# Request, selection and accumulator stores moved in the seam before the first expert of a hybrid encoder layer

## The chip, the cores and the metric

The kernel runs on one core of a Trainium2 chip. Its engines work side by side, each through its own list of instructions, and wait for one another through semaphores: PE (TensorE, the matrix multiplications), DVE (VectorE) and ACT (ScalarE, both elementwise), POOL (GpSimd, used here for small work and for transfers whose rows are chosen by an index), and SP (SyncE, which does nothing here but issue transfers). The profile lists PE's weight loads apart as PEld. The metric is the device time of one execution in microseconds (us), lower is better; where several runs are given, their median counts.

## The reference

One layer of an encoder on 1024 tokens of width 1024, in float32. A mixer (a retention, a state-space and a windowed attention head group) is followed by a layer norm, a layer of 16 experts that choose their tokens, and a second layer norm:

```python
mix = concat(retention, s5, attention) @ w_out
h = layer_norm(ALPHA * h + mix, ln1_g, ln1_b)         # "H1" below
ffn = expert_choice_ffn(h, router_w, w_gate, w_up, w_down)
h = layer_norm(ALPHA * h + ffn, ln2_g, ln2_b)

def expert_choice_ffn(x, router_w, w_gate, w_up, w_down):
    cap = EC_FACTOR * seq // N_EXPERTS                 # 128 tokens for each expert
    aff = softmax(x @ router_w)                        # tokens x 16 experts
    gates, idx = lax.top_k(aff transposed, cap)        # each expert takes its best 128
    xs = x[idx]
    hdn = silu(xs @ w_gate) * (xs @ w_up)              # 128 x 2048
    out = (hdn @ w_down) * gates
    return zeros.at[idx].add(out)                      # summed by token
```

## The kernel before

The tokens are eight tiles of 128 rows (0 to 7; the code calls 7 `LT`, the last tile). A front of some 448 us computes the mixer and the first norm tile by tile; the experts follow, one after another, each in four quarters of its 2048 hidden columns.

**What sets the order.** The whole kernel is scheduled by hand. A table, `ENDS` (for the last tiles; `PLACES` for the others), gives each step a due time, and `F.at(zero + place, step)` sorts the steps by it. Each engine then takes its instructions in that order. The numbers are due times of the plan, not times of the trace: they set an order and nothing else. Transfers that SP issues keep this order too.

**The norm's end of each tile.** For tile `t` the normed rows `z` are written to DRAM twice: as they are, by `out_proj_store` (`H1`, L1727: `h_d<-z`), from where the experts fetch their tokens; and times ALPHA, by `out_proj_scale` on ACT (`AH`, L1734: `ah<-z`) and `out_proj_scaled` (`AD`, L1738: `acc_d<-ah`), as the start of the accumulator to which the experts add. The buffers come from pools. Tag `z` of pool `op` has three places. In this stretch they hold in turn rows of the last tiles, the `ah` of tiles 6 and 7 and the candidates' rows `xc`. Tile 7's mean and gain are computed in halves (`GH`, `SJ`), and its power (`PW`, L1601 on POOL) gives the reciprocal deviation from which both its rows and its softmax follow.

**The first expert's tokens without a search.** Experts 1 to 15 get their tokens by a search (`top_k`, with L2212 among its lines), which takes long and runs on DVE between the other work of the first expert. Expert 0 gets its own by counting. Of tiles 0 to 6 the best 128 tokens are found ahead of tile 7 ("candidates"): their numbers give an index (`CI`, `candidates_index`, L2106), and POOL fetches their rows by it (`XC`, `candidates_rows`, L2111: `z<-h_d,cindex`, into `xc`). When tile 7's affinities are there, each candidate counts how many of tile 7's tokens go ahead of it (`RD7`, L2046 on DVE; `PC`, `first_counts`, L2153 on PE; `LP` and `U1`, L2169 and L2173 on DVE), and each token of tile 7 gets its rank (`RR`, `LR`, `U0`: L2046, L2049, L2161, L2165 on DVE). `U1` and `U0` leave in `rows` two 128x128 matrices of zeros and ones, `K.hits[1]` for the candidates and `K.hits[0]` for tile 7. `first_turned` (`FZ` with tile 7's rows `z`, `FX` with `xc`) multiplies rows and hits on PE into two halves of PSUM, and so both selects and transposes the expert's tokens: `tp<-rows,z`, two halves of four blocks by two sources, 16 multiplications in all (the trace has two records for each). ACT copies the halves to `xF` (`X0`, `first_tokens`, L2445), which PE multiplies with the first gate weights; `xT`, split in two parts, follows. Between the steps on which PE waits, `idle` puts multiplications whose result nobody reads (`FILL` says behind which step and how many).

**The experts' weights** come in pieces of 1 MB (128x2048). For each quarter SP loads two pieces of the gate, two of the up, and two of the down matrix of the quarter before. Most pieces go to `wraw` (`X.load`, L2379) and are split into a high part by ACT (L2417) and the rest by DVE (L2426), from which PE makes three multiplications in place of one; pieces 0, 1, 4, 5, 10 and 11 go whole to `whole` (`X.load_whole`, L2404) and are multiplied unsplit. `RL` are the loads of pieces 2 and 3, `up` of the first quarter, in the order's words two `wraw<-in_exp_w_up`; `W4` those of 4 and 5.

**Memory taken over.** When the front is done its pools are closed, among them `op` (with tag `z`) and `tk`; in the same memory `ex`, `raw2` and `sel` are opened. `raw2` takes the weight loads from piece 8 on in part, `sel` holds the search's buffers `w`, which two COPY of DVE fill (L2212: `w<-tp`). Whoever writes first into such a buffer waits until the front's instructions, transfers included, that read or wrote that memory are done.

Of the kernel before, what the change touches and what calls it, by code (L numbers as in the profile page):

```python
# [9 lines left out]
F32 = mybir.dt.float32  # L10
# [10 lines left out]
P = 128  # L21
L = 1024
D = 1024
NT = L // P
# [1358 lines left out]
def last_steps(K, last, spaces):  # L1383

    X = K.X
    last("XH", 0, fn=spaces[0], by=-0.0005)
    for i in range(2):
        last("XH", i, fn=lambda i=i: X.high(2 + i))
        last("XL", i, fn=lambda i=i: X.low(2 + i))
    for i in range(2):  # L1390
        last("RL", i, fn=lambda i=i: X.load(2 + i))
    for kind, k in (("W0", 0), ("W4", 4)):
        last(kind, fn=lambda k=k: X.load_whole(k))
    for kind, fn in (("CP", candidates_counts), ("CQ", candidates_sums), ("CR", candidates_ranks), ("CH", candidates_hot),
                     ("CF", candidates_numbers), ("CC", candidates_keep), ("CI", candidates_index),
                     ("XC", candidates_rows), ("CA", candidates_half), ("CB", candidates_share), ("CT", candidates_parts),
                     ("CK", candidates_turn), ("CW", candidates_row), ("TS", silu_table), ("R7", first_row),
                     ("RD7", first_before), ("PC", first_counts), ("RR", first_own), ("LR", first_sum), ("U0", first_hits),
                     ("LP", first_place), ("U1", first_hits_row), ("HB", first_parts)):
        last(kind, fn=lambda fn=fn: fn(K))  # L1400
    last("R7", fn=spaces[1], by=-0.0005)
    K.halves = {}
    for half in range(2):
        last("FZ", half, fn=lambda half=half: first_turned(K, half, 0))
        last("FX", half, fn=lambda half=half: first_turned(K, half, 1))
        last("X0", half, fn=lambda half=half: X.first_tokens(half, K.halves[half]))
    last("FX", 1, fn=lambda: setattr(K, "numbers", first_numbers(K)), by=0.0005)
    for half in range(2):
        last("GH", half, fn=lambda half=half: out_proj_gain(K, LT, half))
        last("SJ", half, fn=lambda half=half: out_proj_shift(K, LT, half))  # L1410
    for kind, n in FILL:
        last(*kind, fn=lambda n=n: idle(K, n), by=0.0004)
# [303 lines left out]
def out_proj_gain(K, t, half=None):  # L1716
    z, cs = out_proj_columns(K, t, half)
    K.nc.vector.scalar_tensor_tensor(z, z, K.mr[t][0], K.g1[:, cs], op0=OP.subtract, op1=OP.mult)


def out_proj_shift(K, t, half=None):
    z, cs = out_proj_columns(K, t, half)
    K.nc.vector.scalar_tensor_tensor(z, z, K.mr[t][1], K.b1[:, cs], op0=OP.mult, op1=OP.add)
# [5 lines left out]

def out_proj_scale(K, t):  # L1730

    late = t >= NT - 2
    K.ah[t] = K.op.tile([P, D], F32, name="ah", tag="z" if late else "rt", bufs=3 if late else 1)
    K.nc.scalar.activation(K.ah[t], K.Y[t][2], AF.Copy, scale=ALPHA)  # L1734


def out_proj_scaled(K, t):
# [59 lines left out]
}  # L1797


FILL = ((("RP", 7, 1), 5), (("PC",), 3))  # L1800
ENDS = {
# [76 lines left out]
}  # L1878
# [2 lines left out]
def attention_steps(K, F, zero, out, qs, mat, spaces):  # L1881
# [26 lines left out]
    for c in range(NT):  # L1908
# [38 lines left out]
        for kind, fn in (("AF", router_logits), ("AE", router_exp), ("AG", router_shares), ("GN", out_proj_gain),  # L1947
                         ("SH", out_proj_shift), ("H1", out_proj_store), ("AH", out_proj_scale), ("AD", out_proj_scaled),
                         ("TK", token_parts), ("RK", rank_turn), ("RW", rank_keep), ("RB", rank_count)):
            if c < LT or kind in ("AF", "AE", "AG", "H1", "AH", "AD", "TK"):  # L1950
                at(c, kind, fn=lambda c=c, fn=fn: fn(K, c))
        if 0 < c < LT - 1:
            at(c, "CN", fn=lambda c=c: rank_sums(K, c))
            at(c, "CE", fn=lambda c=c: rank_sums_keep(K, c))
    last_steps(K, last, spaces)
    for k in range(2):
        F.at(zero + PERIOD * 4 + PLACES["LD"] + 0.01, lambda k=k: X.load(k))
# [50 lines left out]
LT = NT - 1  # L2008
# [166 lines left out]

def first_turned(K, half, i):

    if i == 0:
        K.halves[half] = K.ptp.tile([P, 4, P], F32, name="tp")
    src = (K.Y[LT][2], K.xc)[i]  # L2180
    for c in range(4):
        cs = slice((half * 4 + c) * P, (half * 4 + c + 1) * P)
        K.nc.tensor.matmul(K.halves[half][:, c, :], src[:, cs], K.hits[i], start=(i == c == 0), stop=(i == 1 and c == 3))


def first_parts(K):
# [5 lines left out]
def first_numbers(K):  # L2192

    nc, h = K.nc, K.hitb
    pt = K.ptp.tile([P, 4, P], F32, name="tp")
    nc.tensor.matmul(pt[:, 0, 0:5], h[0], K.tok[:, LT, 0, :], start=True, stop=False)
    nc.tensor.matmul(pt[:, 0, 0:5], h[1], K.cparts, start=False, stop=True)
    return pt
# [345 lines left out]
def idle(K, n):  # L2544

    ps = K.pmm.tile([P, 512], F32, name="gu" if K.pmm is K.__dict__.get("pg") else "mm")
    for i in range(n):
        K.nc.tensor.matmul(ps, K.X.whl[2][:, 0, 0:P], K.X.whl[2][:, 0, 0:512], start=True, stop=True)
# [300 lines left out]
```

## Time and profile before

| | |
|---|---|
| runs of the kernel, median of 3 | 1564.23 us (1562.92 to 1564.55) |
| profiled execution | 1562.62 us |
| its span in the trace | 1560.9 us |
| instructions | 21150 |
| read from memory, written | 461.75 MB, 42.99 MB |
| mean rate over the span | 323 GB/s |
| largest group, PE L2334 `gu<-whl,xT` | 3000 multiplications, 712.5 us busy |
| split of the weights, DVE L2426 | 378, 860.5 us busy, 2288 ns each |
| split of the weights, ACT L2417 | 378, 725.3 us busy, 1919 ns each |

Busy time is the time in which an engine worked, a weight load of PE beside its multiplications apart. A busy share alone says little where the stages have different limits; the chain of waits, followed back from the last instruction, says which engine's work could not have been later. A row of the timeline has the start in us, the busy time, the engine, the line, the operation with output and inputs, and, in brackets, the idle time ahead of it and who ended it. SPq and POOLq are the two queues' issues of transfers, and behind an issue stands the median time to its landing.

### The profile page before, as it was taken

What the parts mean: (1) busy time and instruction counts of PE and PEld (TensorE: products, weight loads), DVE (VectorE), ACT (ScalarE), POOL (GpSimd) and SP (SyncE); (2) the same over time, 40 slices, a digit from 0 to 9 for tenths busy, and PEclk for the clock granted to TensorE, in tenths of its full rate; (3) what the DMA queues carried; (4) which work ended last, traced back from release to release, by engine and by line L of the source; (5) the groups of instructions that cost most, each with busy time, mean ns of one, the idle gap of its engine ahead of it and who ended that gap; (6) DMA issues with size and microseconds to landing.
All of it is one profiled execution on the core that took longest, in us unless ns stands there. A gap on an engine that the chain in (4) does not pass through costs nothing.

```text
span 1560.9 us, 21150 instructions
## 1 busy us (share of the span) xinstructions
PE 1543.1 (99%) x7710; PEld 1262.5 (81%) x7710; DVE 1401.8 (90%) x1720; ACT 1130.7 (72%) x1329; POOL 191.5 (12%) x248
## 2 busy tenths in 40 slices
PE   9999999999999999999999999999999999999997
PEld 7887887888767888888888888888888888888886
DVE  7987965889989999999999999989999999999996
ACT  7746556887736777777777777787877878787773
POOL 4002111111010001010010101000211201021121
PEclk9999999999999999999999999999999999999999
DMA  6556478353179999999999999999999999999992
GB/s 242 185 167 155 119 232 234 102 166 109 72 311 371 373 390 411 427 387 367 392 371 387 371 401 370 403 411 409 421 412 409 415 425 413 417 414 413 402 415 108
DMA packets 105177, 507.20 MB, mean 325 GB/s; under 512 B 16752, under 2 KB 29808, under 8 KB 54640
## 3 DMA queue, kind: packets, MB, share of 16 engines
q1 hardware_dynamic: 88624, 474.81, 77.6%
q0 software_dynamic: 16304, 30.94, 7.2%
q8 instruction: 61, 1.00, 0.2%
q14 instruction: 44, 0.36, 0.1%
q10 hardware_dynamic: 144, 0.09, 0.0%
HBM read 461.75 MB, written 42.99 MB: 323 GB/s over the span
## 4 chain that ended last, share of the span: by engine, by line
PE 90%; ACT 3%; DMA 3%; DVE 2%; issue 1%; POOL 1%; SPq 1%; POOLq 0%; ACTq 0%; DVEq 0%
PE gu L2334 44%; PE y L2334 22%; PE mm L64 4%; PE mm L66 4%; PE mm L65 4%; PE tp L2317 3%; PE gu L2342 1%; PE po L1525 1%; PE tp L1505 1%; DMA wraw<-in_w_out 1%; PE at L1454 1%; PE sm L265 0%; DMA uT<-in_x 0%; ACT S L1497 0%; PE at L699 0%
## 5 line engine op out<-in xcount | busy, mean ns | idle before, releaser
L2426 DVE TENSOR_TENSOR whl<-wraw,whl 128x2048 fp32r<-128x2048 f32 x378 | 860.5, 2288 | 61.1 <-ACT whl L2417 57.1
L2417 ACT ACTIVATE whl<-wraw 128x2048 fp32r<-128x2048 f32 x378 | 725.3, 1919 | 246.3 <-PE gu L2334 132.5
L2334 PE MATMUL gu<-whl,xT 128*128 128x512 f32 x3000 | 712.5, 394 | 0.0
L2334 PEld LDWEIGHTS gu<-whl,xT 128*128 128x128 f32 x3000 | 555.4, 188 | 114.8 <-issue 1.0
L2334 PE MATMUL y<-whl,hT 128*128 128x512 f32 x1536 | 359.4, 389 | 0.0
L2334 PEld LDWEIGHTS y<-whl,hT 128*128 128x128 f32 x1536 | 288.0, 188 | 59.7
L2295 POOL DMA_INDIRECT xs<-h_d,index x15 | 26.7, 1777 | 451.3 <-PE y L2334 304.1
L64 PE MATMUL mm<-hT,whl 128*128 128x512 f32 x160 | 65.3, 408 | 0.0
L66 PE MATMUL mm<-hT,whl 128*128 128x512 f32 x160 | 62.6, 391 | 0.0
L65 PE MATMUL mm<-hT,whl 128*128 128x512 f32 x160 | 62.5, 391 | 0.0
L64 PE MATMUL mm<-WO,yh 128*128 128x512 f32 x128 | 53.4, 418 | 0.0
L56 DVE TENSOR_TENSOR hT<-tp,hT 128x512 fp32r<-128x512 f32 x76 | 51.5, 683 | 1.9 <-ACT hT L55 1.7
L55 ACT ACTIVATE hT<-tp 128x512 fp32r<-128x512 f32 x76 | 43.7, 581 | 12.8 <-PE tp L206 6.7
L66 PE MATMUL mm<-WO,yl 128*128 128x512 f32 x128 | 50.6, 396 | 0.0
L65 PE MATMUL mm<-WO,yh 128*128 128x512 f32 x128 | 50.6, 395 | 0.0
L2468 DVE TENSOR_TENSOR hid<-hid,gu 128x512 f32<-128x512 f32 x64 | 43.5, 680 | 2.0 <-PE gu L2334 2.0
L64 PE MATMUL mm<-whl,hT 128*128 128x256 f32 (+1 forms) x120 | 42.4, 353 | 1.5 <-ACT gate L403 1.5
L2462 ACT ACTIVATE hid<-gu 128x512 f32<-128x512 f32 x64 | 37.1, 580 | 5.7 <-PE gu L2342 5.5
L66 PE MATMUL mm<-whl,hT 128*128 128x256 f32 (+1 forms) x120 | 40.2, 335 | 0.0
L65 PE MATMUL mm<-whl,hT 128*128 128x256 f32 (+1 forms) x120 | 40.0, 333 | 0.0
L1465 DVE CUSTOM_DVE_ANT_0 S<-at,R,sink 128x384 f32<-128x384 f32 (+1 forms) x64 | 36.8, 577 | 2.3 <-PE at L1454 1.7
L2317 PEld LDWEIGHTS tp<-ident,hid 128*128 128x128 f32 x256 | 31.8, 140 | 8.5 <-issue 0.5
(450 smaller groups left out, 1779.4 us busy)
## 6 DMA issues: line engine op xcount, KB each, us to landing
wraw<-in_exp_w_up SPq DMA_DIRECT2D x128, 1024.0 KB, 9.5
wraw<-in_exp_w_down SPq DMA_DIRECT2D x128, 1024.0 KB, 10.2
wraw<-in_exp_w_gate SPq DMA_DIRECT2D x122, 1024.0 KB, 9.2
wraw<-in_w_in SPq DMA_DIRECT2D x6, 1024.0 KB, 5.3
whole<-in_exp_w_gate SPq DMA_DIRECT2D x6, 1024.0 KB, 8.5
q_d<-kst SPq DMA_DIRECT2D x32, 128.0 KB, 2.6
wraw<-in_w_out SPq DMA_DIRECT2D x4, 1024.0 KB, 7.6
qs<-q_d POOLq DMA_DIRECT2D x16, 256.0 KB, 3.4
```

The costliest lines, as they stand in the source:

```text
L55: nc.scalar.activation(hi, src, AF.Copy)
L56: eng.tensor_tensor(lo, src, hi.bitcast(F32), OP.subtract)
L64: nc.tensor.matmul(ps, a[0], b[0], start=start, stop=False)
L65: nc.tensor.matmul(ps, a[0], b[1], start=False, stop=False)
L66: nc.tensor.matmul(ps, a[1], b[0], start=False, stop=stop)
L1465: K.nc.vector.tensor_tensor_reduce(S[g][:, :W], K.at.pop((i, g))[:, :W], K.R[:, ro:ro + W], 2.0 ** -(h + 1), K.sink[:, h:h + 1], OP.add, O ...
L2317: K.nc.tensor.transpose(pt[:, c, :], src[:, (c0 + c) * P:(c0 + c + 1) * P], K.ident)
L2334: nc.tensor.matmul(ps, a[s][c], u[:, t, i * w:(i + 1) * w], start=first and id(ps) not in began, stop=last and left[id(ps)] == 0)
L2417: self.K.nc.scalar.activation(u[:, 0, :], self.raw[k1].rearrange("p a b -> p (a b)"), AF.Copy)
L2426: self.K.nc.vector.tensor_tensor(u[:, 1, :], raw, u[:, 0, :].bitcast(F32), OP.subtract)
L2462: nc.scalar.activation(self.h[q], self.pg[q][0], AF.Silu)
L2468: at(self.after, q, 3, lambda: nc.vector.tensor_tensor(self.h[q], self.h[q], self.pg[q][1], OP.mult))
```

## The change

Four things move; no arithmetic is added or left out. (1) The request for the candidates' rows (`XC`) and its index (`CI`) go ahead of tile 7's power. (2) The candidates' count, place and hits go ahead of tile 7's rank on DVE, and PE multiplies the candidates first: `FX` opens each PSUM group and `FZ` closes it. One idle multiplication is left in place of three. (3) `AH` of tile 6 scales its rows in place instead of into a buffer of tag `z`, and its store goes behind tile 7's rows. (4) `AH` and `AD` of tile 7 go behind the loads `RL` and `W4`.

```diff
-    last("FX", 1, fn=lambda: setattr(K, "numbers", first_numbers(K)), by=0.0005)
+    last("FZ", 1, fn=lambda: setattr(K, "numbers", first_numbers(K)), by=0.0005)
...
 def out_proj_scale(K, t):
-    late = t >= NT - 2
-    K.ah[t] = K.op.tile([P, D], F32, name="ah", tag="z" if late else "rt", bufs=3 if late else 1)
+    if t == LT - 1:
+        K.ah[t] = K.Y[t][2]
+    else:
+        K.ah[t] = K.op.tile([P, D], F32, name="ah", tag="z" if t == LT else "rt", bufs=3 if t == LT else 1)
     K.nc.scalar.activation(K.ah[t], K.Y[t][2], AF.Copy, scale=ALPHA)
...
-FILL = ((("RP", 7, 1), 5), (("PC",), 3))
+FILL = ((("RP", 7, 1), 5), (("PC",), 1))
...
-    "AH": {6: 287.000, 7: 375.566},
-    "AD": {6: 315.900, 7: 378.895},
+    "AH": {6: 287.000, 7: 470.000},
+    "AD": {6: 336.001, 7: 470.100},
...
-    "XC": 335.142,
+    "XC": 279.500,
...
-    "FX": (378.883, 389.769),
+    "FX": (335.610, 335.620),
...
 def first_turned(K, half, i):
-    if i == 0:
+    if i == 1:
         K.halves[half] = K.ptp.tile([P, 4, P], F32, name="tp")
     src = (K.Y[LT][2], K.xc)[i]
     for c in range(4):
         cs = slice((half * 4 + c) * P, (half * 4 + c + 1) * P)
-        K.nc.tensor.matmul(K.halves[half][:, c, :], src[:, cs], K.hits[i], start=(i == c == 0), stop=(i == 1 and c == 3))
+        K.nc.tensor.matmul(K.halves[half][:, c, :], src[:, cs], K.hits[i], start=(i == 1 and c == 0), stop=(i == 0 and c == 3))
```

The other entries of `ENDS` that change (`CI`, `PC`, `LP`, `U1`) are seen in the order. The first place is DVE between tile 7's softmax (`aff<-aff,rsm`) and the first split of a weight piece; `G` and `cnt` are the comparisons and their counts, `last` the ranks, `rows` the hits. Before:

```order
L1708 TENSOR_SCALAR aff<-aff,rsm 128x16
L2046 TENSOR_SCALAR G,cnt<-rows,aff 128x128
L2046 TENSOR_SCALAR G,cnt<-tp,aff 128x128
L2049 SCALAR_TENSOR_TENSOR junk,cnt<-tp,aff,upto 128x128
L2161 TENSOR_REDUCE last<-cnt 128x1
L2165 TENSOR_SCALAR rows<-slots,last 128x128
L2169 SCALAR_TENSOR_TENSOR last<-tp,place 128x1
L2173 TENSOR_SCALAR rows<-slots,last 128x128
```

With the change, at the same place (the lines after it are two higher):

```order
L1708 TENSOR_SCALAR aff<-aff,rsm 128x16
L2048 TENSOR_SCALAR G,cnt<-rows,aff 128x128
L2171 SCALAR_TENSOR_TENSOR last<-tp,place 128x1
L2175 TENSOR_SCALAR rows<-slots,last 128x128
L2048 TENSOR_SCALAR G,cnt<-tp,aff 128x128
L2051 SCALAR_TENSOR_TENSOR junk,cnt<-tp,aff,upto 128x128
L2163 TENSOR_REDUCE last<-cnt 128x1
L2167 TENSOR_SCALAR rows<-slots,last 128x128
```

The candidates' place and hits moved ahead of tile 7's own four instructions. On POOL the request `z<-h_d,cindex` changed places with the power `l1rs<-l1rs,mhalf` and now stands ahead of it.

The second place is SP's list of transfers at the end of the front; the first row is tile 6's row store. Before:

```order
L1727 DMA h_d<-z 128x1024
L2404 DMA whole<-in_exp_w_gate 128x2048 x2
L1738 DMA acc_d<-ah 128x1024
L1727 DMA h_d<-z 128x1024
L1738 DMA acc_d<-ah 128x1024
L2379 DMA wraw<-in_exp_w_up 128x2048
L2404 DMA whole<-in_exp_w_gate 128x2048 x2
L2379 DMA wraw<-in_exp_w_up 128x2048
L2379 DMA wraw<-in_exp_w_down 128x2048 x2
```

With the change (tile 6's store now reads `z`, which it was scaled into):

```order
L1727 DMA h_d<-z 128x1024
L2406 DMA whole<-in_exp_w_gate 128x2048 x2
L1727 DMA h_d<-z 128x1024
L1740 DMA acc_d<-z 128x1024
L2381 DMA wraw<-in_exp_w_up 128x2048
L2406 DMA whole<-in_exp_w_gate 128x2048 x2
L2381 DMA wraw<-in_exp_w_up 128x2048
L1740 DMA acc_d<-ah 128x1024
L2381 DMA wraw<-in_exp_w_down 128x2048 x2
```

Tile 6's store went behind tile 7's row store, and tile 7's went from ahead of the four pieces of 1 MB to behind them.

The third place is DVE at the first two COPY of the search, with what they wait for; `w` are the search's buffers, `slotc` and `gates` the first expert's numbers. Each transfer has a semaphore that stands for it: SP's are DMAHW0 to DMAHW7 in turn, POOL's DMASW0 to DMASW7. In the program of before, the COPY's DMAHW4 is tile 7's store of L1738, DMAHW2 tile 6's, and DMAHW3 tile 7's row store. Before:

```order
L2307 TENSOR_TENSOR slotc<-slotc 128x1
L2308 TENSOR_TENSOR gates<-slotc 128x1 [waits DVE_49]
L2212 COPY w_5382<-tp 128x64 [waits DMAHW4_49,DMAHW5_49,DMAHW3_49,DMAHW6_49,DMAHW2_49,DMAHW7_49,DMASW4_49,PE_49]
L2212 COPY w_5384<-tp 128x64
L2215 MAX half_5386<-w_5382 128x8 [waits DVE_49]
```

With the change, DMAHW0 is tile 7's store of L1740, DMAHW3 tile 6's and DMAHW2 tile 7's row store:

```order
L2309 TENSOR_TENSOR slotc<-slotc 128x1
L2310 TENSOR_TENSOR gates<-slotc 128x1 [waits DVE_49]
L2214 COPY w_5379<-tp 128x64 [waits DMAHW3_49,DMAHW5_49,DMAHW2_49,DMAHW6_49,DMAHW0_49,DMAHW7_49,DMASW4_49,PE_49]
L2214 COPY w_5381<-tp 128x64
L2217 MAX half_5383<-w_5379 128x8 [waits DVE_49]
```

The COPY waits for tile 7's store in both programs; what moved is where that store stands on SP. SP's first load behind the store, `wraw<-in_exp_w_down`, waits for the same store in both.

8 rows, old and new, of the table ENDS are left out of this document.

## The prediction

> **What bounds the kernel now.** I read the page's busy times and its chain of waits, then the busy times by stretch, then the timelines of the five engines and the DMA landings around 440 to 480 us, where the change sits.
>
> ```profile
> PE 1543.1 (99%) x7710; PEld 1262.5 (81%) x7710; DVE 1401.8 (90%) x1720; ACT 1130.7 (72%) x1329; POOL 191.5 (12%) x248
> PE 90%; ACT 3%; DMA 3%; DVE 2%; issue 1%; POOL 1%; SPq 1%; POOLq 0%; ACTq 0%; DVEq 0%
> 600.00:700.00 100.00, 100.00 (x480) 82.18 (x479) 92.72 (x66) 76.75 (x55) 9.90 (x4) 1.00 1.01 405
> ```
>
> TensorE bounds it. In the last row (a stretch of the experts; the columns are the stretch, its length, busy PE, PEld, DVE, ACT and POOL, clock, DMA share, GB/s) PE has no free microsecond. So whatever PE loses before or early in the experts stays lost to the end, and whatever it gains is kept only if DVE (93%) and DMA (1.01) follow.
>
> The seam before the first expert, on PE and DVE:
>
> ```profile
> 442.63 0.18 PE L2153 MATMUL tp<-order,G 128*128 128x1 bf16 x1
> 442.68 1.45 PE L2548 MATMUL gu<-whl 128*128 128x512 f32 x3
> 444.06 4.09 PE L2183 MATMUL tp<-rows,z 128*128 128x128 f32 x32
> 448.04 3.68 PE L2342 MATMUL gu<-whole,xF 128*128 128x512 f32 x8
> 438.01 0.16 DVE L2116 TENSOR_TENSOR cand<-cand 128x1 f32<-128x1 f32 x1
> 438.28 0.15 DVE L2106 TENSOR_TENSOR cindex<-cand 128x1 uint32<-128x1 f32 x1
> 442.22 0.35 DVE L2046 TENSOR_SCALAR_CACHE_REDUCE G<-rows,aff 128x128 bf16<-128x128 f32 x1
> 443.71 0.29 DVE L2165 TENSOR_SCALAR rows<-slots,last 128x128 f32<-128x128 f32 x1
> 444.10 0.29 DVE L2173 TENSOR_SCALAR rows<-slots,last 128x128 f32<-128x128 f32 x1
> 445.09 0.75 DVE L1723 SCALAR_TENSOR_TENSOR z<-z,l1rs,b 128x512 f32<-128x512 f32 x1
> ```
>
> PE counts (442.63), fills with three idle multiplications, and starts the 16 selecting ones at 444.06, when the last tile's selection (443.71 + 0.29) is there. They take 4.0 us; the first expert starts at 448.04.
>
> **The candidates' rows and the selection (the gain).**
>
> ```profile
> 439.55 0.98 POOL L1601 TENSOR_TENSOR l1rs<-l1rs,mhalf 128x1 f32<-128x1 f32 x1 [6.45 <-DVE l1rs L1595]
> 440.72 1.08 POOL L2111 DMA_INDIRECT z<-h_d,cindex  x1 [0.18 <-DMA whole<-in_exp_w_gate]
> z<-h_d,cindex POOLq DMA_INDIRECT x1, 4.4
> L2295 POOL DMA_INDIRECT xs<-h_d,index x15: 938/1036/3062, 496.3 to 1396.8; - x15
> ```
>
> The index takes the slot at 438.01 instead of 438.28, and the gather no longer queues behind the power (439.55 to 440.53). It starts near 438.3, 2.4 us sooner, and with its 4.4 us lands near 442.7 instead of 445.1. POOL is free again at 438.3 + 1.08 = 439.4, just before the power's operand arrives at 439.5; I cost that at nothing. With the longest such request (3.06 us, third figure of the last row) the power would be 1.8 us late, and the softmax, queued on DVE behind it, too.
>
> Selecting the candidates first: the count ends at 442.81, the place and its selection follow on DVE and end near 443.4, so PE starts 0.6 us sooner (443.45 for 444.06). The last tile's selection comes 0.7 us later than now, about 444.4, behind eight multiplications that last to 445.4; its second half of rows (445.09 + 0.75 = 445.84) is needed near 446.5. Both are covered. The two idle multiplications that go were waiting time. But the clock (columns after the busy time: clock, DMA share, GB/s) was at half there:
>
> ```profile
> 440.38:440.50 0.12, 0.12 (x1) 0.50 0.00 0
> 443.75:443.88 0.12, 0.12 (x2) 0.85 0.80 328
> 1550.67:1551.10 0.43, 0.03 (x1) 1.00 0.00 0
> 1553.24:1553.66 0.43, 0.00 (x0) 0.50 0.00 0
> ```
>
> It fell near 440.4 and was back near 443.8, 3.4 us later, although the fillers ran. The 0.35 us from 443.45 to 443.8 at half speed give back 0.2, so the first expert starts **0.4 us sooner**, near 447.6.
>
> **The accumulator stores (the loss).** Tile 6's scaling in place costs the same 1.05 us; tile 7's now stands on ACT between xF and xT, and xT, 0.5 us later, is still done four microseconds before its first use. What counts is where the stores stand on SP's queue.
>
> ```profile
> 440.22 0.33 SPq L1738 DMA_DIRECT2D acc_d<-ah  x1
> 445.87 0.33 SPq L1727 DMA_DIRECT2D h_d<-z  x1
> 447.00 0.96 SPq L1738 DMA_DIRECT2D acc_d<-ah  x1
> 448.01 0.43 SPq L2379 DMA_DIRECT2D wraw<-in_exp_w_up  x1
> 449.89 0.66 SPq L2379 DMA_DIRECT2D wraw<-in_exp_w_up  x1
> 451.30 1.08 SPq L2379 DMA_DIRECT2D wraw<-in_exp_w_down  x2
> acc_d<-ah SPq DMA_DIRECT2D x1, 512.0 KB, 4.2
> wraw<-in_exp_w_up SPq DMA_DIRECT2D x1, 1024.0 KB, 13.3
> out<-zz SPq DMA_DIRECT2D x8, 512.0 KB, 9.3
> 445.92 1.06 ACT L1734 ACTIVATE ah<-z 128x1024 f32<-128x1024 f32 x1 [1.19 <-DVE z L1723]
> 448.19 0.60 ACT L2445 ACTIVATE xF<-tp 128x512 f32<-128x512 f32 x1 [0.72 <-PE tp L2197]
> 463.20 1.91 ACT L2417 ACTIVATE whl<-wraw 128x2048 fp32r<-128x2048 f32 x1 [5.50 <-DMA wraw<-in_exp_w_up]
> 465.84 1.91 ACT L2417 ACTIVATE whl<-wraw 128x2048 fp32r<-128x2048 f32 x1 [0.73 <-DMA wraw<-in_exp_w_down]
> ```
>
> Tile 7's store was issued at 447.00, ahead of four 1 MB loads, and landed 4.2 us later, at 451.2. Two things wait for that landing, because their buffers lie where the front's pools were: SP's next load (451.30) and the first COPY of the top-k search on DVE (the order's third place: its store semaphore is now DMAHW0). Now the store is issued only after all four loads, near 449.5 (ACT: second xF until 448.4, then 1.06). When does it land? The load issued at 449.89 landed 13.3 us later, at 463.2; it had the same bytes ahead of it as now (tile 6's store takes tile 7's place). With 0.5 MB more at 2.64 us per MB (463.20 to 465.84) the store lands 1.3 us behind it; up to 0.7 goes back because tile 6's store follows the row store at once: 463.8 to 464.5. As the loads behind it are now held back and do not share the engines, I take **463.5**. Ends: 449.5 + 4.2 = 453.7 if it landed as now, 449.5 + 9.3 = 458.8 as the late output stores do with loads ahead of them, and 464.5. It is nearest to the 13.3 us row, which is the same queue at the same moment.
>
> What stands behind the COPY:
>
> ```profile
> 451.87 0.22 DVE L2212 COPY w<-tp 128x64 f32<-128x64 f32 x1 [0.71 <-PE tp L2208]
> 460.79 0.69 DVE L2468 TENSOR_TENSOR hid<-hid,gu 128x512 f32<-128x512 f32 x1
> 465.14 2.29 DVE L2426 TENSOR_TENSOR whl<-wraw,whl 128x2048 fp32r<-128x2048 f32 x1 [2.03 <-ACT whl L2417]
> 464.02 0.60 PE L2317 MATMUL tp<-ident,hid 128*128 128x128 f32 x4
> 478.90 0.24 PE L2238 MATMUL tp<-ident,b 32*128 32x32 f32 x1
> ```
>
> From the COPY to the end of `hid` DVE works 451.87 to 461.48, 9.6 us, without a wait. PE transposes `hid` at 464.02: 2.5 us of slack, and the COPY comes 11.7 us later. PE starts that transpose at 463.5 + 0.1 + 9.6 + 0.1 = 473.3, **9.3 us later** than now (458.8 would give 4.6; 464.5, 10.3; 453.7, nothing). The 0.4 us gained are swallowed by this wait. Behind it DVE loses its 2.03 us idle at 465.14, so it is 9.6 us late at 478.90, no more than PE. The loads that SP holds go out at 463.6; the piece at 451.30 took 14.5 us to 465.84, so even so it is split by 482.3, and PE wants the rest of it near 484.
>
> PE idles from 463.6 to 473.3. At the end of the kernel the clock fell 2.5 us after PE's last work, and at 440.4 it took 3.4 us of work to return. I add half of 3.4, **1.7 us** (0 if it stays up, 3.4 if it takes two such spans).
>
> Sum: 9.3 + 1.7 = 11.0. The profiled execution took 1562.6 (span 1560.9 and 1.7 around it): 1573.6. The runs' median lies 1.6 above it, so **1575.2**.
>
> The Trainium skill, "TensorE: Matmul & The Clock Gate", Part 1, says the clock is set by free-running windows of about 3.4 us and returns after one busy window. By that rule the restart runs at half speed for one to two windows, 1.7 to 3.4 us lost, and the sum would be 1575.2 to 1576.9; the 3.4 us seen at 440.4 agree with it.
>
> **The rivals.**
> - *The store passes the loads* and lands 4.2 us after its issue, at 453.7. Then the COPY is 1.9 us late, DVE's `hid` ends at 463.4, in time for PE at 463.6, and DVE's idle 2.03 us take up the rest. Only the early selection counts: 1564.2 - 0.4 = 1563.8, not slower. It decides below a landing of 453.9. For it: stores landed in 4.2 us. Against it: the output stores' 9.3 us and the load's 13.3. Chance 0.07.
> - *The gather holds POOL* for 3.06 us. The softmax, the row store and all of SP's queue behind it come 1.8 us late: 1577.0, inside the range; with the long clock loss 1578.7, above it. Against it: 1.08 us there now, and a median of 1.04. Chance 0.08.
> - *The store lands between*, 455 to 458.8: 1566 to 1569.7. Chance 0.04.
>
> The Trainium skill, "DMA: Bandwidth & Descriptors", section "Queues, rings and completion order", says that each DMA engine takes descriptors in ring order, though a later DMA may complete first. By the first half the store waits for the loads and the sum stands at 1575.2; by the second half alone the time would be the first rival's 1563.8. The 9.3 us row agrees with the first half.
>
> **How the numbers follow.** The forecast has 0.81, the rivals 0.07, 0.08 and 0.04. The range runs from a landing at 458.8 with half the clock loss (4.6 + 0.9: 1569.7) to 464.5 with the long one (10.3 + 3.4: 1577.9). A difference of 0.2%, 3.1 us, is about what a measurement of this kernel tells from no change. Slower by more: 0.91; within: 0.07; faster by more: 0.02.
>
> **What would show it.** Right: the gather starts near 438.3 and PE's selecting multiplications near 443.4; acc_d<-ah is issued near 449.5 with over 12 us to landing; DVE's first COPY of the top-k stands still for some 12 us, released by that DMA; PE idles 8 to 10 us before the first `hid` transpose, and its clock reads 0.50 there. Wrong: a store that lands before 454, or a COPY that starts near 452; then the time is near 1564.

## The result, and the profile after

| | before | changed |
|---|---|---|
| median of 6 runs each | 1564.25 us | 1575.39 us (1574.60 to 1576.58) |
| ratio, 95% interval | | 1.0074 (1.0063 to 1.0084) |
| profiled execution, its span | 1562.62, 1560.9 us | 1576.58, 1574.8 us |

The change costs 11.1 us by the medians, where 11.0 was forecast. The two profiled executions lie 13.9 us apart: before's is shorter than its median by 1.6, the changed kernel's is the longest of its six. First the page of the changed kernel, busy times and shares of the chain:

```profile
PE 1544.4 (98%) x7708; PEld 1261.6 (80%) x7708; DVE 1401.4 (89%) x1720; ACT 1130.6 (72%) x1329; POOL 194.9 (12%) x248
PE 87%; DVE 4%; DMA 4%; ACT 3%; issue 1%; POOL 1%; SPq 0%; POOLq 0%; ACTq 0%; DVEq 0%
```

PE did the same work. Its share of the chain fell from 90% to 87%, and DVE and DMA gained what it lost. Where, the waits between 448 and 476 us say (who waited for what: us in total, times, longest):

```profile
DVE w L2214 <- DMA acc_d<-ah: 13.1, 1, 13.1
PE tp L2319 <- DVE hid L2470: 10.6, 1, 10.6
```

And the chain that ended last, in the same stretch:

```profile
450.80 13.86 DMA acc_d<-ah
...
464.83 0.36 DVE w L2214 x2
465.19 0.26 DVE half L2217 x2
...
471.58 2.20 DVE whl L2428
473.78 0.61 DVE hid L2470
474.39 0.04 issue
474.44 1.11 PE tp L2319 x4
```

It reads from top to bottom: tile 7's accumulator store is under way for 13.9 us, then DVE begins the search, works through it and the split behind it, multiplies `hid`, and only then PE can transpose it. SP's issues show the other waiter:

```profile
446.73 0.35 SPq L1740 DMA_DIRECT2D acc_d<-z  x1
...
449.94 0.76 SPq L2381 DMA_DIRECT2D wraw<-in_exp_w_up  x1
450.80 0.59 SPq L1740 DMA_DIRECT2D acc_d<-ah  x1
464.83 0.81 SPq L2381 DMA_DIRECT2D wraw<-in_exp_w_down  x2
```

The next load goes out at 464.83, at the instant of DVE's COPY: one landing releases both.

To place the 13.9 us, I cut each trace at four of PE's instructions: the router's first multiplication of the last tile, the first expert's first work, the first transpose of `hid`, and the turn of the search's result. Their starts before (the third and fourth, 464.02 and 478.90, stand in the prediction):

```profile
438.45 0.96 PE L1656 MATMUL sm<-rwg,rt 128*128 128x16 f32 x8
447.99 0.17 PE L2196 MATMUL tp<-tok,hitb 128*128 128x5 bf16 x1
```

and in the changed kernel, with the selection and what follows the wait:

```profile
438.79 0.96 PE L1656 MATMUL sm<-rwg,rt 128*128 128x16 f32 x8
444.00 3.81 PE L2185 MATMUL tp<-rows,z 128*128 128x128 f32 x32 [0.42 <-DMA z<-h_d,cindex]
447.64 0.17 PE L2198 MATMUL tp<-tok,hitb 128*128 128x5 bf16 x1
474.44 1.11 PE L2319 MATMUL tp<-ident,hid 128*128 128x128 f32 x4 [10.62 <-DVE hid L2470]
475.35 5.94 PE L2344 MATMUL gu<-whole,xF 128*128 128x512 f32 x8
492.12 0.25 PE L2240 MATMUL tp<-ident,b 32*128 32x32 f32 x1
```

The differences of these starts, for every kernel of this study (us; A, from the router to the first expert; B, on to the `hid` transpose; C, on to the search's turn):

| trace | A | B | C | A+B+C against before | time of the runs, against before |
|---|---|---|---|---|---|
| before | 9.54 | 16.03 | 14.88 | | |
| changed | 8.85 | 26.80 | 17.68 | +12.9 | +11.1 |
| e1_store_alone | 9.62 | 23.64 | 16.49 | +9.3 | +9.7 |
| e2_store_early | 9.42 | 16.02 | 14.88 | -0.1 | +0.5 |
| e3_own_place | 8.69 | 16.00 | 15.11 | -0.6 | -0.6 |
| e4_other_queue | 8.95 | 20.91 | 17.11 | +6.5 | +6.2 |
| e5_filled_wait | 8.82 | 25.36 | 14.95 | +8.7 | +11.6 |
| e6a_three_ahead | 8.88 | 23.16 | 16.57 | +8.2 | +9.1 |
| e6b_one_ahead | 8.73 | 18.46 | 16.60 | +3.3 | +4.4 |
| e7_search_apart | 8.94 | 16.02 | 17.23 | +1.7 | +3.3 |
| f1_changed_again | 8.80 | 26.59 | 17.70 | +12.6 | +10.6 |
| f2_filled_again | 8.78 | 25.37 | 14.94 | +8.6 | +8.2 |
| f3_gather_late | 12.31 | 16.03 | 14.88 | +2.8 | one run |
| f4_store6_early | 11.23 | 16.04 | 14.88 | +1.7 | one run |

From the search's turn to the end of the span all of them need 1082.0 to 1082.7 us. So the change gains 0.7 us in A and loses 10.8 in B and 2.8 in C. The rest of the 13.9 us between the two profiled executions (0.3 ahead of A, 0.7 behind C) is no larger than such differences between traces. What lies ahead of the seam differs among the traces by up to 6.5 us (the router's first multiplication starts between 437.99 and 444.46), in steps that no edit here touches; that is why a difference of one or two us between the last two columns says nothing, and why the stretches are read.

### The profile page after: what moved, and what is told of

Its sections match the earlier page's. It is cut to its first block, busy times and chain, and to the rows that moved or that the text cites. A ratio compares the mean times of both kernels' runs of the same rounds, so it can differ in the third digit from the quotient of the medians.

```text
span 1574.8 us, 21148 instructions
## 1 busy us (share of the span) xinstructions
PE 1544.4 (98%) x7708; PEld 1261.6 (80%) x7708; DVE 1401.4 (89%) x1720; ACT 1130.6 (72%) x1329; POOL 194.9 (12%) x248
## 4 chain that ended last, share of the span: by engine, by line
PE 87%; DVE 4%; DMA 4%; ACT 3%; issue 1%; POOL 1%; SPq 0%; POOLq 0%; ACTq 0%; DVEq 0%
PE gu L2336 42%; PE y L2336 21%; PE mm L64 4%; PE mm L66 4%; PE mm L65 4%; PE tp L2319 3%; DMA acc_d<-ah 1%; PE po L1525 1%; PE tp L1505 1%; PE at L1454 1%; PE gu L2344 1%; DMA wraw<-in_exp_w_down 1%; DMA wraw<-in_exp_w_gate 1%; DVE whl L2428 1%; DMA wraw<-in_w_in 1%
## 5 line engine op out<-in xcount | busy, mean ns | idle before, releaser
L2297 POOL DMA_INDIRECT xs<-h_d,index x15 | 30.9, 2057 | 463.0 <-PE y L2336 305.1
L2319 PE MATMUL tp<-ident,hid 128*128 128x128 f32 x256 | 38.9, 274 | 10.6 <-DVE hid L2470 10.6
L2464 ACT ACTIVATE hid<-gu 128x512 f32<-128x512 f32 x64 | 37.2, 581 | 12.6 <-PE gu L2344 12.4
```

The source lines that it names most:

```text
L2297: K.nc.gpsimd.indirect_dma_start(out=xs, out_offset=None, in_=K.h1_dram, in_offset=bass.IndirectOffsetOnAxis(ap=K.index[:, e:e + 1], axis=0))
L2319: K.nc.tensor.transpose(pt[:, c, :], src[:, (c0 + c) * P:(c0 + c + 1) * P], K.ident)
L2464: nc.scalar.activation(self.h[q], self.pg[q][0], AF.Silu)
```

## The experiments

**Is it the late store alone?** The kernel before, with tile 7's two steps late and nothing else:

```diff
-    "AH": {6: 287.000, 7: 375.566},
-    "AD": {6: 315.900, 7: 378.895},
+    "AH": {6: 287.000, 7: 470.000},
+    "AD": {6: 315.900, 7: 470.100},
```

> The kernel before with one part of the change only: AH and AD of tile 7 at 470.0 and 470.1, behind the four 1 MB loads. If the late store alone makes the loss: about 1575.5 us, 11 to 11.5 above before (the same landing near 464.8, the same wait of DVE's first COPY of the search, PE idle about 10 us ahead of the first hid transpose); the 0.3 us of the other parts were swallowed by that wait anyway. If the loss needs the in-place scaling, the earlier gather or the missing fillers: 1564 to 1566.

Measured: 1573.66 us (4 runs, 1571.63 to 1575.01), ratio 1.0063 (1.0043 to 1.0083). DVE's COPY:

```profile
461.64 0.36 DVE L2212 COPY w<-tp 128x64 f32<-128x64 f32 x2 [9.92 <-DMA acc_d<-ah]
```

The same wait with the same releaser, so the store alone makes the loss, 9.7 of the 11.1 us; the rival's 1564 to 1566 is out. It came 2 us below the forecast. Here tile 6's store still goes ahead of the last tile's rows, the four loads start 1.3 us sooner, and the store, issued at 449.37, lands 12.1 us later, 3.2 us ahead of the change's. B is 3.2 us shorter than in the change. That part (3) makes part (4) dearer by so much is not shown: in the experiments below, traces with the change's own order of transfers differ among themselves by 1.4 us in this landing.

**Is the rest harmless?** The changed kernel with both lines of the first diff as they were before:

> The changed kernel with AH and AD of tiles 6 and 7 at their old places, all else as changed. If the late store is the whole loss: 1563.9 us, because the first expert starts 0.3 us sooner than before (447.7 for 448.04 in the traces), within 0.2% of before. If gather, selection, in-place scaling or fillers carry a part of the loss: between 1566 and 1575.

Measured: 1564.43 us (12 runs), ratio 1.0001 (0.9991 to 1.0011). B and C are those of before. The loss is gone, and of the 0.7 us in A almost all too (9.42), as the request for the candidates' rows took 5.0 us to land here; the last two experiments come back to that.

**Waits, or the store's place in the queue?** The store stays as late, but `ah` of tile 7 lies elsewhere, in the place that the low part of the next expert's tokens takes later:

```diff
-        K.ah[t] = K.op.tile([P, D], F32, name="ah", tag="z" if t == LT else "rt", bufs=3 if t == LT else 1)
+        K.ah[t] = (K.xt.tile([P, D], F32, name="ah", tag="xT1", bufs=2) if t == LT else
+                   K.op.tile([P, D], F32, name="ah", tag="rt", bufs=1))
```

> The changed kernel, its store just as late and in the same place of SP's queue, but ah of tile 7 lies in the free second place of xT's low part, outside the memory that the search and the next loads take over. If the two waits for the landing are the loss: the store still lands 13 to 14 us after its issue, the COPY starts near 452 and SP's next load near 452, and the time is 1563.9 to 1564.5 us. If the store's place in the queue, its bytes among the loads or the delay of the loads by it are the loss: about 1575 us.

Measured: 1563.30 us (12 runs), ratio 0.9996 (0.9984 to 1.0007). The transfer issued at 451.25, with the time to its landing:

```profile
acc_d<-ah SPq DMA_DIRECT2D x1, 512.0 KB, 12.7
```

and DVE's COPY:

```profile
452.11 0.36 DVE L2215 COPY w<-tp 128x64 f32<-128x64 f32 x2
```

The store lands nearly as late as in the change (12.7 us after its issue, where 13 to 14 were expected), and nobody waits for it: COPY at 452.11, the next load at 451.99, B 16.00. Here the late landing costs nothing by itself; the two waits made the loss. This is the change without its fault. Its seam is 0.6 us shorter than before's, which the runs' interval can't tell from none.

**Which of the two waits?** A stretch of memory that nobody writes pushes the search's buffers beyond the pool of `ah`; the COPY is freed and SP's load is not:

```diff
+    c_pad, pad = pool("pad")
+    level(pad, 15968)
     c_sel, K.sel = pool("sel")
...
-        close(c_sel)
+        close(c_sel, c_pad)
```

> The changed kernel with an unused stretch of memory ahead of the search's buffers, so that they lie beyond the pool of ah: DVE's COPY no longer waits for the store, SP's next load still does. If the COPY's wait carries the loss: the COPY starts near 452, PE does not idle at the first hid, and the time is 1564 to 1566 us, though SP's loads are held until 464.8. If the held loads carry it: near 1575 us; in between, the share of each.

Measured: 1567.52 us (10 runs), ratio 1.0023 (1.0013 to 1.0033); seam +1.7. The time is above the 1564 to 1566 of the first case. The COPY starts at 454.78 without a wait (the front of this trace is 3.3 us longer than before's), and B is 16.02, so the whole 10.8 us of B is the COPY's. But C is 17.23, and PE's row there shows why:

```profile
483.96 0.21 PE L2240 MATMUL tp<-ident,b 32*128 32x32 f32 x1 [1.93 <-DVE b L1972]
```

The held loads arrive late, ACT and DVE split them late, and the search behind those splits on DVE comes 1.9 us late for PE. So SP's wait is worth about 2.4 us in C where PE is on time (in this one trace, in which the clock did not fall); I had expected nothing. In the change PE is 10 us late by then, and C has another cause, which the filled wait shows.

**Behind the loads, or among them?** The same late store, issued from ACT's own queue:

```diff
-    K.nc.sync.dma_start(K.acc_dram[t * P:(t + 1) * P, :], K.ah.pop(t))
+    (K.nc.scalar if t == LT else K.nc.sync).dma_start(K.acc_dram[t * P:(t + 1) * P, :], K.ah.pop(t))
```

> The changed kernel, tile 7's late store issued from ACT's own queue in place of SP's; buffer and waits for it as changed. If the store is late because it stands behind the 4 MB of loads in one queue: it lands 4 to 9 us after its issue near 449.5, at 454 to 459, and the time is 1564 to 1569 us. If it is late because the 16 engines are busy with the loads whatever the queue: it lands near 463 and the time is near 1575 us.

Measured: 1570.12 us (7 runs), ratio 1.0040 (1.0027 to 1.0053). The store, with the time to its landing:

```profile
acc_d<-ah ACTq DMA_DIRECT2D x1, 512.0 KB, 9.3
```

9.3 us to the landing, where SP's queue took 12.7 (e3) to 13.9 (the change) and, in the kernel before, with no load ahead of the store, 4.2: neither theory alone. Of a delay of 8.5 to 9.7 us, 5.1 remain when the store shares the 16 engines with the loads from another queue, and 3.4 to 4.6 belong to the place behind 4 MB in one queue.

**How much for each megabyte?** Fewer of the four loads ahead of the store; in e6a the second up piece goes behind it, in e6b both gate pieces too:

```diff
-    "RL": (381.347, 388.699),
+    "RL": (381.347, 470.200),
```

```diff
-    "W4": 388.566,
+    "W4": 470.200,
-    "RL": (381.347, 388.699),
+    "RL": (381.347, 470.300),
```

> The changed kernel with the second up load of the first quarter behind tile 7's store: 3 MB of loads stand ahead of the store, not 4. If the landing follows the bytes ahead in the queue: it lands 2.6 us sooner, near 462, the COPY and PE's wait are 2.6 us shorter, and the time is near 1572.8 us. If it does not depend on them: 1575.4.

> The changed kernel with only 1 MB ahead of tile 7's store (both gate pieces and the second up piece go behind it). If the landing follows the bytes ahead: near 455, the COPY 3 us late and PE less than 1 us, time 1564 to 1566 us; the gate pieces are issued 2 us later, and PE may wait 1 to 2 us for them at 460. If it does not depend on them: 1575.

Measured: 1573.27 us (1.0064, 1.0046 to 1.0082) and 1568.62 us (1.0021, 1.0011 to 1.0030). The landings in e6a:

```profile
acc_d<-ah SPq DMA_DIRECT2D x1, 512.0 KB, 11.2
```

and in e6b:

```profile
acc_d<-ah SPq DMA_DIRECT2D x1, 512.0 KB, 6.8
```

With 0, 1, 3 and 4 MB ahead the landing took 4.2, 6.8, 11.2 and 13.9 us: 2.4 us for each MB (2.1 if 4 MB are counted with e3's 12.7), somewhat less than the 2.64 us from load to load by which the prediction reckoned. e6a's landing and time came near the forecast. e6b was forecast at 1564 to 1566 and missed: its landing took 6.8 us, so PE waited 2.3 us and not under 1, and its clock fell at the end of that wait (C 16.60). Its ten runs lie in two groups, four at 1565.5 to 1566.2 us and six at 1568.4 to 1570.8; the trace is of the slowest, and what the four did otherwise is not known.

**What does the clock cost?** Ten idle multiplications ahead of the first `hid` transpose:

```diff
+        if q == 0:
+            at(self.before, *turn, lambda: idle(K, 10))
         at(self.before, *turn, put("tp", lambda: turned(K, self.h[q], 0)))
```

> The changed kernel with 10 idle multiplications of 0.9 us (first tokens by the first gate weights, result read by nobody) on PE ahead of the first hid transpose, where it waits 10.6 us; it adds work and removes none. If the half clock after the wait costs time: PE's clock stays at 1.00, the first transposes take 0.60 us in place of 1.11 and the next eight gate multiplications 3.6 in place of 5.9, and the time falls by 1.7 to 2.8 us, to 1572.6 to 1573.7. If the clock costs nothing in the median run: 1575.4 or a little more.

Measured: 1575.76 us (4 runs, 1572.81 to 1579.71), by which the clock would cost nothing. The trace says otherwise: C is 14.95, as before. Its front was 3.7 us longer than before's, so it was measured again beside the changed kernel, five runs each:

> The changed kernel once more, beside the filled wait on the same chip: 1575.4 us, and in its trace the same 2.8 us between the first hid transpose and the search's last turn (17.7 us for 14.9 before) if PE's clock fell in the wait.

> The kernel of e5 (idle multiplications in PE's wait) again, beside the changed kernel. If the clock costs what the traces showed (2.8 us): 2 to 3 us below f1. If it costs half of that in the median of runs: 1 to 2 us below. If the loss at half clock only appears in the profiled execution: the same as f1 within 0.5 us.

Measured: f1 1574.95 us (1574.06 to 1581.44; ratio 1.0065, 1.0052 to 1.0079), f2 1572.58 us (1570.93 to 1574.35; 1.0050, 1.0036 to 1.0063). PE in f2:

```profile
465.63 8.75 PE L2554 MATMUL gu<-whole,xF 128*128 128x512 f32 x20
474.96 0.66 PE L2319 MATMUL tp<-ident,hid 128*128 128x128 f32 x4 [0.58 <-DVE hid L2470]
475.45 3.60 PE L2344 MATMUL gu<-whole,xF 128*128 128x512 f32 x8
```

With PE kept at work the eight gate multiplications take 3.60 us, in the change 5.94, and C is 14.94: in these traces the clock carries C's loss, and the held loads none of it. Other traces agree. Wherever the clock fell in PE's wait, it stayed at half for some us after PE's restart, and C lost half of that time (us):

| trace | PE's wait | half clock after the restart | C lost |
|---|---|---|---|
| changed | 10.6 | 5.6 | 2.8 |
| f1 | 10.4 | 5.7 | 2.8 |
| e4 | 4.7 | 4.5 | 2.2 |
| e6b | 2.3 | 3.4 | 1.7 |
| e6a | 7.0 | 3.3 | 1.7 |
| e1 | 7.5 | 3.2 | 1.6 |

In e1, for example, where PE restarts at 471.25 (the third figure from the right is the clock):

```profile
471.25:474.40 3.15, 3.15 (x7) 1.93 (x8) 3.01 (x9) 0.60 (x1) 0.00 (x0) 0.50 1.02 432
474.45:476.00 1.55, 1.55 (x5) 0.70 (x4) 1.48 (x7) 0.00 (x0) 0.00 (x0) 1.00 1.01 428
```

The length of the wait does not set the loss: 2.3 us of it cost as much as 7. By the mean clocks it fell in every run of the changed kernel, not only in the traced ones: the mean of its six runs and of f1's five is 0.993 to 0.995, that of the nine runs with the filled wait 0.997 to 0.998, that of the kernel before 0.996 to 0.998. (0.004 less over 1575 us is, by estimate, 13 us at half clock; the trace has it low from 466.4 to 480.1.) The medians of f1 and f2 differ by 2.4 us. That is not the clock alone, though, since the two traces differ by 4.0: 2.8 in C and 1.2 in B, because the store landed sooner in f2. In f1:

```profile
acc_d<-ah SPq DMA_DIRECT2D x1, 512.0 KB, 13.7
```

and in f2:

```profile
acc_d<-ah SPq DMA_DIRECT2D x1, 512.0 KB, 12.5
```

The transfers ahead of the store are the same, and the idle multiplications come after its landing. Both traces of the changed kernel have 13.7 to 13.9 us, those of e3, e5, e7 and f2 12.5 to 12.7; why is open.

**What made the gain in A?** Both in the kernel of e3: the request behind the power again, and tile 6's store ahead of the last tile's rows again.

```diff
-    "XC": 279.500,
+    "XC": 335.142,
```

> The kernel of e3 with the request for the candidates' rows behind the power again (POOL starts it 1.1 us later), all else alike. Measured in the trace from the router's first multiplication to the first expert's first work, which took 9.54 us before, 8.85 in the change and 8.69 in e3. If the sooner request carries the gain: 9.6 to 9.8. If the order of selection carries it alone: 8.7 to 8.9.

```diff
-    "AD": {6: 336.001, 7: 470.100},
+    "AD": {6: 315.900, 7: 470.100},
```

> The kernel of e3 with tile 6's accumulator store at its old place, ahead of the last tile's rows, where it is issued less than 1 us after the request for the candidates' rows. Same stretch as in f3. If that store slows the request, as e2's 9.42 us with both stores early may mean: 9.2 to 9.5. If e2's stretch was longer because of tile 7's early scaling: 8.7.

Measured, one run each: A 12.31 and 11.23 us (1568.43 and 1566.81 us). PE in f3:

```profile
448.54 0.80 PE L2186 MATMUL tp<-rows,z 128*128 128x128 f32 x4 [2.35 <-DMA z<-h_d,cindex]
```

the request in f4 (it took 4.2 us in e3 and 4.4 in the change):

```profile
z<-h_d,cindex POOLq DMA_INDIRECT x1, 5.2
```

and a stretch of f4's selection (busy times, then clock, DMA share and GB/s):

```profile
447.00:450.00 3.00, 3.00 (x14) 3.00 (x15) 2.96 (x3) 0.50 (x2) 0.00 (x0) 0.50 0.36 142
```

Both were slower than either theory had it. The candidates-first order can't start before the request has landed; without the sooner request PE starts 2.0 us later than in e3, 7.0 us behind the router's first multiplication, where the kernel before starts after 5.6. With tile 6's store issued 1.1 us behind the request's start, the landing takes 1.0 us longer than in e3 (5.2 for 4.2; 5.0 in e2, which has the store there too), and PE starts that much later. On top of it PE's clock fell in both for 3.4 us, and the selection took 5.3 us from its start to the first expert, where it took 3.65 in e3 and the change; without these 1.6 us f4 would have come near its 9.2 to 9.5. So in these traces, one of each, the gain hangs on the sooner request and on no store just behind it, and the reordering alone loses.

## Why the prediction was right, point by point

- **The gain.** The first expert was forecast near 447.6 and started at 447.64. Two of its steps were off. The request started at 439.43, not near 438.3. In the changed kernel DVE wrote the index

```profile
438.35 0.16 DVE L2108 TENSOR_TENSOR cindex<-cand 128x1 uint32<-128x1 f32 x1
```

and POOL sent the request:

```profile
439.43 1.08 POOL L2113 DMA_INDIRECT z<-h_d,cindex  x1 [6.00 <-DVE l1st L1586]
```

  POOL was free and still began 0.9 us after the index was written. The bracket names a DVE instruction that ended just before the start, but the request did not wait for it: the last of its three waits in POOL's queue begins at 438.6, and as the long one of 7.2 us began earlier, it took 43 ns (their durations in ns, then the first and the last start):

```profile
L2113 POOLq EVENT_SEMAPHORE  x3: 43/43/7220, 431.2 to 438.6; - x3
```

  The trace of before shows nearly the same at the next expert, which I had not read: the index there, on DVE,

```profile
495.38 0.16 DVE L2305 TENSOR_TENSOR index<-slotc 128x1 uint32<-128x1 f32 x1
```

and its request on POOL are 0.8 us apart:

```profile
496.30 0.98 POOL L2295 DMA_INDIRECT xs<-h_d,index  x1 [52.63 <-DVE gates L2308]
```

  So the selection waited for the request's landing and began at 444.00, not 443.45. The selection gave that back, by luck: it was forecast at 4.15 us (443.45 to 447.6) and took 3.64. Of the difference 0.2 is the half clock that I had there, as the clock did not fall in this trace's seam. The other 0.3 I had overlooked. The kernel before, whose clock was back before its selection began, took 3.93; there the candidates' rows landed at 445.1 (440.72 + 4.4), 1.0 us into the selection, and in the changed kernel they have landed when it starts. That this is the 0.3 is likely, but no run isolates it. Against the router's first multiplication the first expert is 0.7 us sooner.
- **The landing.** The wait is the one forecast, on the COPY and on SP's load. The store was issued at 450.80, not 449.5, as SP was still issuing the loads (449.94 + 0.76); it landed at 464.7 for 463.5. That is the term that was short, by 1.2 us, or by 0.8 if the 0.3 of this trace's longer front is taken off. The 13.9 us from issue to landing are as forecast (14.0); what was missed is the moment of the issue. The rival in which it passes the loads is out, and so is the landing in between.
- **DVE's 9.6 us** from the COPY to the end of `hid`: 464.83 to 474.39, 9.56. PE was to be 9.3 us late and was 10.4 (474.44 against 464.02), which is the landing's 1.2 within 0.1.
- **The clock** was put at 1.7 us, half of 3.4. The changed kernel by stretch (columns as in the prediction, the third figure from the right is the clock):

```profile
463.80:465.80 2.00, 0.02 (x1) 0.00 (x0) 0.97 (x9) 1.58 (x1) 0.00 (x0) 1.00 0.06 10
465.80:474.40 8.60, 0.00 (x0) 0.00 (x0) 8.46 (x50) 3.32 (x2) 0.00 (x0) 0.54 0.98 390
474.40:480.80 6.40, 6.36 (x13) 3.20 (x13) 6.16 (x18) 1.10 (x2) 0.00 (x0) 0.56 1.01 426
480.80:482.00 1.20, 1.20 (x6) 0.84 (x5) 1.20 (x2) 0.68 (x2) 0.00 (x0) 1.00 1.10 362
```

  PE's last work ended at 463.8, and the clock fell near 466.4; from 474.4 on a mean of 0.56 over 6.4 us is half speed for 5.6 of them: 2.8 us lost in the trace. So the term was 1.1 short. The Trainium skill, "TensorE: Matmul & The Clock Gate", Part 1, has it that the clock returns after one whole busy window of about 3.4 us; by an estimate from that figure a restart costs half of one to two windows, 1.7 to 3.4 us. The 2.8 agree with it, and the 1.6 to 2.8 of the six traces do within 0.1.
- **SP's held loads** cost nothing in the change, as forecast: the pieces were wanted later because PE was late already. The first row above shows the DMA engines at 0.06 for 2 us while SP waited, and e7 shows the 2.4 us that it costs when PE is on time.
- **The sum.** 11.0 us forecast, 11.1 by the medians. By the trace the seam lost 12.9: counted from the router, the landing was 0.8 us short, the clock 1.1. The medians of both pairs (11.1, and 10.6 for f1) are lower than their traces' 12.9 and 12.6. The traced run was the longest of its group in both. No trace shows a median execution, so where the others saved those 2 us stays open; a sooner landing in those runs, as the 1.2 us in f2's trace, could be a part of it. The mechanism was right; that the time agrees to 0.2 us is luck.

## What to carry to other kernels

Before a store is moved back in a queue, ask who waits for its landing, not who waits for its data: a buffer in memory that a later stage takes over makes that stage's first writer wait, and then everything queued behind that writer. Either keep such a store ahead of the big loads, or give its source a place that nobody takes over soon; then its lateness is free, as in e3. And a saving of half a microsecond ahead of a stage is worth nothing if the same edit puts a transfer on that stage's first wait.

## What the runs showed of the hardware that was not expected

- POOL's indexed request began 0.8 to 0.9 us after its index was written, with POOL idle. It landed 4.2 us after its start in e3 and 4.4 in the change, and 5.0 (e2) and 5.2 (f4) with a 512 KB store issued 1.1 us behind it.
- A 512 KB store behind loads in one queue landed 2.1 to 2.4 us later for each MB; from another queue beside 4 MB of loads still 9.3 us after its issue. With the same transfers ahead of it, it landed after 12.5 to 13.9 us.
- After a wait of PE in which its clock fell, the work behind it lost 1.6 to 2.8 us, half of the time for which the clock stayed low, whether the wait was 2.3 or 10.6 us long. Idle multiplications in the wait kept the clock up.
- The half clock fell into the selection in some traces (f3, f4: 5.3 us) and not in others (the change, e2, e3: 3.65).
